# Down projection of a conv-gated FFN: fourteen of twenty-two tiles as seven block products

## The chip, the cores and the metric

The kernel runs on one core of a Trainium2 chip. The metric is device time in microseconds from launch to end, lower is better; it is given as the median of three runs. One further execution was taken with the hardware profiler, and every duration below that is not such a median is from it.

## The reference, cut to what matters

A two-layer encoder trunk over 1040 frames (16 learned ones ahead of 1024) of width 1024, all in float32. Each layer is an attention part (gated linear attention and softmax attention) and a gated FFN with a causal convolution of width 3. The change is in the FFN's last product:

```python
def conv_ffn(x, w_up, conv_w, conv_b, w_down):
    h = x @ w_up
    L = h.shape[1]
    hp = jnp.pad(h, ((0, 0), (CONV_W - 1, 0), (0, 0)))
    hc = conv_b
    for j in range(CONV_W):
        hc = hc + hp[:, j:j + L] * conv_w[j]
    u, g = jnp.split(hc, 2, axis=-1)
    return (jax.nn.silu(g) * u) @ w_down
...
        h = h + conv_ffn(rms_norm(h, ffn_norm[i]), w_up[i], conv_w[i], conv_b[i], w_down[i])
    return rms_norm(h, final_norm)[:, N_META:]
```

The FFN's inner width is 22 x 128 = 2816. The last layer needs only the last 1024 frames of the down projection.

## The kernel before, in words

Everything is held transposed: 128 channels on the partitions, frames along the row. A float32 product is three matmuls (`mm3`, L212): every operand is split into a rounded part `hi` and a remainder `lo`, and the passes are hi x hi (L216), lo x hi (L217) and hi x lo (L218). The rounded part is a copy on ScalarE (ACT), the remainder a subtraction on VectorE (DVE): for plain weights in `weights` (L183, L185), for activations in `split` (L330, L331). The first pass of a weight needs its `hi` alone, the second needs its `lo`.

The up projection (`ffn_up`, L1017) already is made of block products. Frames are cut in two halves, channels in two halves, and a pair of output tiles (an `u` and a `g` tile) with the two halves of the frames is a two by two block product, done by Winograd's form with seven products in place of eight. Each product has a weight factor (A11, A12, A21, A22 or a sum of them: S1, S2 and the changed A21, A12), made in `up_operand` and split in `up_split` (L1013, L1014), and an activation factor made once per layer. A product is 4 k tiles x 3 passes x 2 column blocks = 24 matmuls of 260 columns (258 in layer 1), into a PSUM tile of two banks. `evacuate` (L1180, L1181) copies or adds products into `u` and `g`; after the seventh, `conv` (L1169, L1173) and the gate (L1198, L1202) make the tile's activation, which POOL's queue stores to DRAM as `actd[j]` (L1203).

The down projection before is plain. `FGROUPS` cuts the 22 k tiles in groups of 5, 5, 5, 4 and 3. For each group but the last, `stream` goes over the eight output tiles m, loading and splitting the weights one tile ahead, and `dense3` makes the product into PSUM tiles of one bank, in chunks of 400, 384 and 256 frames (two of 512 in layer 1). DVE adds each chunk to the residual tile `hT[m]` (L1249), which was loaded from DRAM (`hm`) at the start of the stage (L1363) and stays on chip. `load_act` (L1231) loads an activation from `actd` and splits it. Ten are loaded while the last up tile's products run, by `during_last`, the others two groups ahead. The last group of three (`down_last`, L1261) goes chunk by chunk and feeds the next layer's norm, or the output.

Tiles as wide as a row come from a pool of 33 slots (`Slots`, L54), with six more in the FFN and some of the down stage. A slot is handed out again in the order in which slots were given back; whoever writes a slot next waits until its last user, a transfer included, is done.

PE's order is the order in which the program is written (`manual_schedule`, for PE alone). For the other engines and the queues a scheduler sets the order when the program is built. Each engine and each queue then works strictly in its order: an instruction that waits holds back those behind it.

Of the kernel before, what the change touches and what calls it, by code (L numbers as in the profile page):

```python
# [23 lines left out]
T = META + SEQ  # L24
# [8 lines left out]
CH_DOWN = [(16, 512), (528, 512)]  # L33
CTILES = [(0, 4), (4, 7), (7, 9)]
FT, NT, FIRST = 116, 9, 112
CH_FOX = [(0, 344), (344, 348), (692, 348)]
# [17 lines left out]
class Slots:  # L54
# [22 lines left out]
    def put(self, *slots):  # L77
        for s in slots:
            self.free.append(s.id)
# [53 lines left out]
class Kern:  # L133
# [843 lines left out]


    def up_operand(self, lyr, j, p, fw, raws, odd):
        nc = self.nc  # L980
        if j == 2 and p in (1, 2):
            src = fw.tile([128, 4, 128], F32, tag="raw2", name="raw2")
            nc.sync.dma_start(src[:], self.wm[lyr, M_UP + 4][:, 4 * p - 4:4 * p, :])
            return self.up_split(src, fw, odd)
        if j not in raws:
            u, g = self.wm[lyr, M_UP + 2 * j], self.wm[lyr, M_UP + 2 * j + 1]
            q = raws[j] = {}
            for name, src, k0, own in (("A11", u, 0, True), ("A21", g, 0, False), ("A22", g, 4, False), ("A12", u, 4, True)):
                q[name] = self.wp.tile([128, 4, 128], F32, tag="raw", name="raw", bufs=4) if own else \
                    fw.tile([128, 4, 128], F32, tag="raw2", name="raw2")  # L990
                nc.sync.dma_start(q[name][:], src[:, k0:k0 + 4, :])
        q = raws[j]

        def combine(out, a, b, op):
            if out not in q:
                q[out] = fw.tile([128, 4, 128], F32, tag="raw2", name="raw2")
            nc.vector.tensor_tensor(out=q[out][:], in0=q[a][:], in1=q[b][:], op=op)
# [8 lines left out]
        return self.up_split(src, fw, odd)  # L1006

    def up_split(self, src, fw, odd):
# [4 lines left out]
        nc.scalar.copy(hi[:], src[:])  # L1013
        nc.vector.tensor_tensor(out=lo[:], in0=src[:], in1=hi[:].bitcast(F32), op=ALU.subtract)  # L1014
        return [(hi[:, k, :], lo[:, k, :]) for k in range(4)]

    def ffn_up(self, lyr, mix, hT, pp, fw, halves, o0, during_last):  # L1017
        nc, s = self.nc, self.slots
# [218 lines left out]
        s.put(t)  # L1237
        acts[j] = (ah, al)

    def down_tiles(self, lyr, hT, pp, o0, dchunks, acts):  # L1240
        nc, s = self.nc, self.slots

        def down(i, m):
            g0, ng = FGROUPS[i]

            def f(w):
                def ev(ps, c0, n):
                    h = hT[m][:, c0:c0 + n]
                    nc.vector.tensor_tensor(out=h, in0=ps, in1=h, op=ALU.add)  # L1249
                self.dense3(pp, w, [acts[j] for j in range(g0, g0 + ng)], dchunks, ev)  # L1250
                if m == KD - 1:
                    for j in range(g0, g0 + ng):
                        s.put(*acts.pop(j))
                    if i + 2 < len(FGROUPS):
                        a, b = FGROUPS[i + 2]
                        for j in range(a, a + b):
                            self.load_act(j, o0, acts)
            return (self.wd[lyr, m][:, g0:g0 + ng, :], f)
        return [down(i, m) for i in range(len(FGROUPS) - 1) for m in range(KD)]

    def down_last(self, lyr, hT, pp, dchunks, acts, at_end, es):  # L1261

        nc, s = self.nc, self.slots
        g0, ng = FGROUPS[-1]
        w, held = [], []
        for m in range(KD):
            if m % 2 == 0:
# [55 lines left out]
    def run(self):  # L1323
# [17 lines left out]
        for lyr in range(DEPTH):  # L1341
            last = lyr == DEPTH - 1
            chunks = CH_LAST if last else CH
            mix, hT = self.attention(lyr, nm, hsrc, chunks, feed)
            o0 = CH_OUT[0][0] if last else 0
            dch = CH_OUT if last else CH
            acts, early = {}, {1: 2, 6: 2, 2: 1, 7: 2, 5: 1, 4: 1, 3: 1}

            def during_last(p):
                for _ in range(early[p]):  # L1350
                    self.load_act(len(acts), o0, acts)
# [82 lines left out]
```

## Time and profile before

| | us |
|---|---|
| median of three runs | 2647.05 |
| lowest and highest | 2646.37, 2649.61 |
| the profiled execution | 2645.09 |
| its span, first to last instruction | 2643.3 |
| mean granted TensorE clock | 0.987 |
| layer 0: first matmul of the down stage, first of its last group | 1071.76, 1288.92 |
| layer 1: the same | 2380.23, 2591.48 |

PE is TensorE's matmuls, PEld its weight loads, DVE VectorE, ACT ScalarE, POOL GpSimd, SP SyncE, whose queue issues most loads. In the busy times, a count follows each engine. In the groups of instructions a row is: line, engine, operation, output <- inputs, shapes, count | busy us, mean ns of one | idle time of the engine before them and what ended it. In the timeline a row is: start, duration in us, engine, line, operation, tiles, count, and in brackets the idle time before with what ended it. Matmuls overlap, so a matmul's own duration says less than the distance between the starts of two.

### The profile page before, as it was taken

Reading aid. Unit: us, or ns where it says so; the run is one execution under the profiler, and the core shown is the slowest. Engines: PE = TensorE matmul, PEld = TensorE weight load, DVE = VectorE, ACT = ScalarE, POOL = GpSimd, SP = SyncE. Lnnn points to the kernel's source line nnn. Section 1 sums busy time; section 2 is a strip of 40 time slices with the busy share of each in tenths; the row PEclk is TensorE's granted clock in tenths of the full one; section 3 lists DMA queues with packets and bytes.
Section 4 is the critical chain, followed back from the end, with each engine's and each line's share of the span. In section 5 each row is a group of like instructions: output and inputs, shape, how many; then the busy total and the mean of one; then the engine's idle time right before and its main releaser. Section 6 shows DMA issues by size and latency. Waiting matters only on the chain.

```text
span 2643.3 us, 46336 instructions
## 1 busy us (share of the span) xinstructions
PE 2523.9 (95%) x18102; PEld 2407.2 (91%) x18102; DVE 1759.9 (67%) x3484; ACT 1240.1 (47%) x2677; POOL 457.9 (17%) x596
## 2 busy tenths in 40 slices
PE   8999999897999999999999999998989999999997
PEld 7988898897999999999999888887889999998886
DVE  7655676759877777643665666666698767776335
ACT  6345665645544445421343565665455444453112
POOL 4033333333000000000201333332320000000002
PEclk9999999998999999999999999999999999999999
DMA  3222124341222222632312222142512222245222
GB/s 125 65 83 70 47 83 124 106 131 58 97 81 76 85 77 92 217 94 58 103 56 65 75 72 74 56 138 91 158 51 85 83 81 77 83 139 189 65 55 77
DMA packets 114476, 240.72 MB, mean 91 GB/s; under 512 B 14432, under 2 KB 36192, under 8 KB 114256
## 3 DMA queue, kind: packets, MB, share of 16 engines
q1 hardware_dynamic: 96000, 182.27, 22.7%
q0 software_dynamic: 16384, 53.18, 5.5%
q8 instruction: 142, 2.33, 0.4%
q10 hardware_dynamic: 1872, 2.31, 0.2%
q14 instruction: 78, 0.64, 0.1%
HBM read 174.01 MB, written 50.91 MB: 85 GB/s over the span
## 4 chain that ended last, share of the span: by engine, by line
PE 77%; DVE 13%; ACT 4%; issue 3%; DMA 2%; POOL 2%; DVEq 0%; SPq 0%; POOLq 0%; ACTq 0%
PE mm L216 12%; PE mm L217 12%; PE mm L218 12%; PE up L216 10%; PE up L217 10%; PE up L218 10%; PE av L706 2%; PE tr L688 2%; DVE S L655 1%; DVE x L1038 1%; PE wo L217 1%; PE wo L216 1%; PE wo L218 1%; DVE PT L331 1%; ACT P L667 1%
## 5 line engine op out<-in xcount | busy, mean ns | idle before, releaser
L216 PE MATMUL up<-x,hi 128*128 128x260 f32 (+1 forms) x2464 | 701.3, 285 | 22.7 <-DVE hu L1180 20.3
L217 PE MATMUL up<-x,lo 128*128 128x260 f32 (+1 forms) x2464 | 699.2, 284 | 0.0
L218 PE MATMUL up<-x,hi 128*128 128x260 f32 (+1 forms) x2464 | 698.5, 283 | 0.0
L216 PEld LDWEIGHTS up<-x,hi 128*128 128x128 f32 x2464 | 467.5, 190 | 24.4 <-DVE hu L1180 20.7
L217 PEld LDWEIGHTS up<-x,lo 128*128 128x128 f32 x2464 | 467.9, 190 | 0.1
L218 PEld LDWEIGHTS up<-x,hi 128*128 128x128 f32 x2464 | 467.8, 190 | 0.0
L216 PE MATMUL mm<-xh,hi 128*128 128x348 f32 (+4 forms) x1056 | 365.1, 346 | 0.0
L218 PE MATMUL mm<-xl,hi 128*128 128x348 f32 (+4 forms) x1056 | 340.9, 323 | 0.0
L217 PE MATMUL mm<-xh,lo 128*128 128x348 f32 (+4 forms) x1056 | 340.8, 323 | 0.0
L1014 DVE TENSOR_TENSOR lo<-raw,hi 128x512 fp32r<-128x512 f32 x308 | 212.9, 694 | 146.2 <-ACT hi L1013 146.2
L183 ACT CAST hi<-raw 128x512 fp32r<-128x512 f32 (+1 forms) x264 | 142.3, 543 | 329.8 <-PE mm L218 240.0
L217 PE MATMUL mm<-ah,lo 128*128 128x400 f32 (+1 forms) x760 | 266.4, 351 | 0.2 <-DVE lo L185 0.2
L218 PE MATMUL mm<-al,hi 128*128 128x400 f32 (+1 forms) x760 | 265.9, 350 | 0.0
L216 PE MATMUL mm<-ah,hi 128*128 128x400 f32 (+1 forms) x760 | 265.8, 350 | 0.0
L185 DVE TENSOR_TENSOR lo<-raw,hi 128x512 fp32r<-128x512 f32 (+1 forms) x196 | 120.7, 620 | 181.1 <-ACT hi L183 177.5
L1013 ACT CAST hi<-raw 128x512 fp32r<-128x512 f32 x308 | 190.3, 620 | 107.6 <-PE up L218 92.7
L216 PEld LDWEIGHTS mm<-xh,hi 128*128 128x128 f32 x1056 | 201.0, 190 | 6.0 <-issue 5.3
L217 PEld LDWEIGHTS mm<-xh,lo 128*128 128x128 f32 x1056 | 200.9, 190 | 0.4 <-issue 0.3
L218 PEld LDWEIGHTS mm<-xl,hi 128*128 128x128 f32 x1056 | 199.9, 189 | 0.4 <-issue 0.3
L1203 POOL DMA_DIRECT2D actd<-cv x44 | 23.4, 533 | 830.0 <-DVE cv L1202 830.0
L667 ACT ACTIVATE P<-S,m 116x460 f32<-116x460 f32 (+2 forms) x224 | 124.8, 561 | 76.9 <-DVE m L655 72.6
L331 DVE TENSOR_TENSOR PT<-tr,PT 116x464 fp32r<-116x464 f32 (+3 forms) x240 | 122.1, 516 | 55.8 <-ACT PT L330 54.1
(248 smaller groups left out, 5269.0 us busy)
## 6 DMA issues: line engine op xcount, KB each, us to landing
raw<-in_wm_dram SPq DMA_DIRECT2D x328, 256.0 KB, 2.6
raw<-in_wd_dram SPq DMA_DIRECT2D x64, 256.0 KB, 2.6
actd<-cv POOLq DMA_DIRECT2D x22, 520.0 KB, 2.9
st<-actd SPq DMA_DIRECT2D x22, 520.0 KB, 4.9
actd<-cv POOLq DMA_DIRECT2D x22, 512.0 KB, 3.0
st<-actd SPq DMA_DIRECT2D x22, 512.0 KB, 4.8
cb<-cd SPq DMA_DIRECT2D x16, 520.0 KB, 4.2
kA<-kA SPq DMA_DIRECT2D x24, 260.0 KB, 3.8
```

Of the source, the lines that this page charges most:

```text
L183: nc.scalar.copy(hi[:, :n, :], raw[:, :n, :])
L185: eng.tensor_tensor(out=lo[:, :n, :], in0=raw[:, :n, :], in1=hi[:, :n, :].bitcast(F32), op=ALU.subtract)
L216: nc.tensor.matmul(ps, wh, xh[:, c0:c0 + n], start=first, stop=False, skip_group_check=more)
L217: nc.tensor.matmul(ps, wl, xh[:, c0:c0 + n], start=False, stop=False, skip_group_check=more)
L218: nc.tensor.matmul(ps, wh, xl[:, c0:c0 + n], start=False, stop=last, skip_group_check=more)
L331: nc.vector.tensor_tensor(out=lo, in0=src, in1=hi.bitcast(F32), op=ALU.subtract)
L655: nc.vector.tensor_tensor_reduce(out=S[:rows, :n], in0=S[:rows, :n], in1=cb[:rows, c0:k1], scale=1.0, scalar=(BIG if ci == 0 else m[:rows, ...
L667: nc.scalar.activation(P[:rows, :n], S[:rows, :n], AF.Exp, scale=-1.0, bias=m[:rows, nch - 1:nch], accum_out=(den if nch == 1 else d3[:row ...
L688: nc.tensor.transpose(tr[:w, j, :rows], P[:rows, o:o + w], id_)
L706: nc.tensor.matmul(av[:, a:width], w.rearrange("p a b -> p (a b)"), x, start=(t == 0 and i == 0), stop=(t == last and i == 1))
L1013: nc.scalar.copy(hi[:], src[:])
L1014: nc.vector.tensor_tensor(out=lo[:], in0=src[:], in1=hi[:].bitcast(F32), op=ALU.subtract)
```

## The change

The fourteen k tiles 3 to 10 and 13 to 18 of the down projection are computed as block products, in two groups of eight and six tiles (`"s"`). Between them two groups of plain tiles remain (`"n"`: 0 to 2 and 11, 12), and the last group, 19 to 21.

- A block group takes pairs of output tiles, the group's first and second half of k tiles, and the two halves of the frames. `block_operand` is `up_operand` made general: four loads of weights, four sums, seven splits a pair. `down_blocks` issues the products in a written order, with the weight factors made four products ahead. A product has 4 (or 3) k tiles x 3 passes x 2 column blocks.
- The seven activation factors of a group are made by `prepare`, a generator that goes on whenever enough slots are free (`pump`, called after each product and each plain tile, and in the last up tile). For each two k tiles of a half it loads four slots, makes four sums and seven splits. The activations of the plain groups are loaded by the same generator.
- All this runs inside the pools of the up stage, with its four PSUM tiles of two banks. A plain tile is now two halves of the frames, each two column blocks of 260 (256 in layer 1), copied from PSUM by ACT into a slot.
- The residual stays in DRAM. Each plain output tile and each finished block tile is added to `hm` by a DMA that accumulates, issued on POOL's queue; `hT` is loaded after the last of them, for the last group.

```diff
-FGROUPS = [(0, 5), (5, 5), (10, 5), (15, 4), (19, 3)]
-HALVES, HALVES_LAST = (0, 520, 520), (8, 524, 516)
+GROUPS, LAST = (("n", 0, 3), ("s", 3, 8), ("n", 11, 2), ("s", 13, 6)), (19, 3)
+HALVES, HALVES_LAST, HALVES_OUT = (0, 520, 520), (8, 524, 516), (16, 528, 512)
...
+    def prepare(self, halves, acts, X):
...
+            nk = ng // 2
+            X[g0] = {p: [] for p in range(1, 8)}
+            for k0 in range(0, nk, 2):
+                m = min(2, nk - k0)
...
+                yield 2 + m
+                a0, a1 = load(g0, 0), load(g0, 1)
+                put(1, a0)
+                yield 2 + m
+                b0, b1 = load(g0 + nk, 0), load(g0 + nk, 1)
+                put(2, b0)
+                yield 1 + m
+                tt(a1, b1, a1, ALU.subtract)
+                t2 = get("t2")
+                tt(t2, a1, a0, ALU.add)
+                put(6, t2)
+                yield m
+                tt(a0, b1, t2, ALU.subtract)
+                put(5, a0)
...
+                put(7, a1)
...
+                tt(b0, b0, t2, ALU.subtract)
...
+                put(4, b0)
...
+                put(3, b1)
+    def pump(self, keep):
+        s = self.slots
+        while self.need + keep <= len([i for i in s.free if i not in s.lent]):
+            self.need = next(self.prep)
...
+    def down_blocks(self, lyr, g0, ng, X, pp, fw, halves, first):
+        seq = [(0, 1)]
+        for j in range(NP):
+            seq += [(j, 2), (j, 6), (j, 5), (j, 7)] + ([(j + 1, 1)] if j + 1 < NP else []) + [(j, 4), (j, 3)]
...
+            elif p == 4:
+                copy(q["g"][:, t0])
+                nc.gpsimd.dma_start(self.hm[2 * j + 1][:, o0:T], q["g"][:, o0:T], accum_op=ALU.add)
+                s.put(q["g"])
+            elif p == 3:
+                add(q["u"][:, t1], q["x"])
+                nc.gpsimd.dma_start(self.hm[2 * j][:, o0:T], q["u"][:, o0:T], accum_op=ALU.add)
+                s.put(q["u"])
...
+    def ffn_down(self, lyr, pp, fw, halves, acts, X, ids):
...
+                for h in range(2):
+                    ps = pp.tile([128, 2, 512], F32, tag=f"p{(2 * m + h) % 4}", name="down", bufs=1)
+                    for k in range(ng):
+                        for c in range(2):
+                            self.mm3(ps[:, c, :n], w[k], acts[g0 + k], halves[h] + c * n, n, k == 0, k == ng - 1)
...
+                        nc.scalar.copy(x, ps[:, :, :n])
+                if kind == "n":
+                    nc.gpsimd.dma_start(self.hm[m][:, o0:T], out[:, o0:T], accum_op=ALU.add)
+                    s.put(out)
...
+                self.pump(3)
...
-                    self.ffn_up(lyr, mix, hT, pp, fw, HALVES_LAST if last else HALVES, o0, during_last)
+                    self.ffn_up(lyr, mix, hT, pp, fw, HALVES_LAST if last else HALVES, o0, lambda p: self.pump(3))
+                    hT = self.ffn_down(lyr, pp, fw, halves, acts, X, ids)
...
-                    hT = [s.get(F32, f"h{k}", first=ids) for k in range(KD)]
-                    for k in range(KD):
-                        nc.sync.dma_start(hT[k][:, o0:T], self.hm[k][:, o0:T])
-                    self.stream(self.down_tiles(lyr, hT, pp, o0, CH_DOWN if last else CH, acts))
```

More of the change, by code (lines that the diff above doesn't have):

```diff
@@ L996, in combine @@
                 q[out] = fw.tile([128, 4, 128], F32, tag="raw2", name="raw2")
-            nc.vector.tensor_tensor(out=q[out][:], in0=q[a][:], in1=q[b][:], op=op)
+            nc.vector.tensor_tensor(out=q[out][:, :nk, :], in0=q[a][:, :nk, :], in1=q[b][:, :nk, :], op=op)
         if p == 6:
@@ new lines, in ffn_down, with load_residual, plain @@
+    def ffn_down(self, lyr, pp, fw, halves, acts, X, ids):
+        nc, s = self.nc, self.slots
+        o0, W = halves[0], halves[2]
+        n = W // 2
+        two = lambda ap: ap.rearrange("p (a b) -> p a b", b=n)
+        hT = []
+        def load_residual():
+            for k in range(KD):
+                hT.append(s.get(F32, f"h{k}", first=ids))
+                nc.sync.dma_start(hT[k][:, o0:T], self.hm[k][:, o0:T])
+        def plain(kind, g0, ng, m):
+            def f(w):
+                out = hT[m] if kind == "r" else s.get(F32, "do")
+                for h in range(2):
+                    ps = pp.tile([128, 2, 512], F32, tag=f"p{(2 * m + h) % 4}", name="down", bufs=1)
+                    for k in range(ng):
+                        for c in range(2):
+                            self.mm3(ps[:, c, :n], w[k], acts[g0 + k], halves[h] + c * n, n, k == 0, k == ng - 1)
+                    x = two(out[:, halves[h]:halves[h] + W])
+                    if kind == "r":
+                        nc.vector.tensor_tensor(out=x, in0=ps[:, :, :n], in1=x, op=ALU.add)
+                    else:
+                        nc.scalar.copy(x, ps[:, :, :n])
+                if kind == "n":
+                    nc.gpsimd.dma_start(self.hm[m][:, o0:T], out[:, o0:T], accum_op=ALU.add)
+                    s.put(out)
@@ L1253, in f @@
                         s.put(*acts.pop(j))
[L1254 to L1257, printed above, removed]
+                self.pump(3)
             return (self.wd[lyr, m][:, g0:g0 + ng, :], f)
-        return [down(i, m) for i in range(len(FGROUPS) - 1) for m in range(KD)]
+        i = 0
+        while i < len(GROUPS):
+            kind, g0, ng = GROUPS[i]
+            i += 1
+            if kind == "r":
+                if not hT:
+                    load_residual()
+                tiles = [plain(kind, g0, ng, m) for m in range(KD)]
+                while i < len(GROUPS) and GROUPS[i][0] == "r":
+                    tiles += [plain(*GROUPS[i], m) for m in range(KD)]
+                    i += 1
+                self.stream(tiles)
+            elif kind == "n":
+                tiles = [plain(kind, g0, ng, m) for m in range(KD)]
+                if i < len(GROUPS) and GROUPS[i][0] == "s":
+                    self.stream(tiles[:-1])
+                    w = self.weights(tiles[-1][0])
+                    _, a, b = GROUPS[i]
+                    i += 1
+                    self.down_blocks(lyr, a, b, X[a], pp, fw, halves, lambda: tiles[-1][1](w))
+                else:
+                    self.stream(tiles)
+        if not hT:
+            load_residual()
+        while any(j not in acts for j in range(LAST[0], sum(LAST))):
+            self.need = next(self.prep)
+        return hT
     def down_last(self, lyr, hT, pp, dchunks, acts, at_end, es):
         nc, s = self.nc, self.slots
-        g0, ng = FGROUPS[-1]
+        g0, ng = LAST
         w, held = [], []
@@ L1346, in run @@
             dch = CH_OUT if last else CH
[L1347 to L1351, printed above, removed]
+            acts, X = {}, {}
+            halves = HALVES_OUT if last else HALVES
+            self.prep = self.prepare(halves, acts, X)
+            self.need = next(self.prep)
             with tc.tile_pool(name=f"ffn{lyr}", bufs=1, reuse_waits="tile") as fp, \
```

108 lines of the change are left out of this document (90 added, 18 removed).

## The prediction

> **What bounds the kernel now.** I read the busy times first, then the granted clock and the busy time of three stretches, then the hand-over from the up stage to the down stage in order of time.
>
> ```profile
> PE 2523.9 (95%) x18102; PEld 2407.2 (91%) x18102; DVE 1759.9 (67%) x3484; ACT 1240.1 (47%) x2677; POOL 457.9 (17%) x596
> PE 77%; DVE 13%; ACT 4%; issue 3%; DMA 2%; POOL 2%; DVEq 0%; SPq 0%; POOLq 0%; ACTq 0%
> ```
>
> ```profile
> core 0: us, PE busy (x) PEld busy (x) DVE busy (x) ACT busy (x) POOL busy (x), PEclk, DMA share, GB/s
> 700.00:1000.00 300.00, 300.00 (x2507) 300.00 (x2506) 220.09 (x284) 144.51 (x209) 7.97 (x15) 1.00 0.24 80
> 1071.76:1288.92 217.16, 216.93 (x1370) 216.62 (x1369) 98.65 (x181) 49.19 (x82) 0.53 (x1) 1.00 0.33 102
> 2380.23:2591.48 211.25, 211.25 (x915) 171.55 (x913) 96.24 (x147) 47.95 (x80) 0.53 (x1) 1.00 0.32 98
> ```
>
> The first stretch is block products of the up stage in layer 0; the next two are the nineteen tiles of the down projection that the change rewrites, from their first matmul to the last group's first. PE is idle 0.23 us in them and has the full clock, while DVE is busy 98.65 of 217.16 us. So the down stage costs what its matmuls cost, and fewer matmul columns are worth their time, as long as PE stays fed.
>
> ```profile
> 1071.64 0.28 PE L218 MATMUL up<-x,hi 128*128 128x260 f32 x1
> 1071.76 0.34 PE L216 MATMUL mm<-ah,hi 128*128 128x400 f32 x1
> 1072.34 0.45 PE L217 MATMUL mm<-ah,lo 128*128 128x400 f32 x1 [0.23 <-DVE lo L185]
> ```
>
> At the hand-over PE waits 0.23 us, for the weight remainder (L185) of the first down tile. This is the wait to watch: the second matmul of each weight needs it.
>
> **The matmul stream.** A block product's matmul takes 300/2507 = 0.1197 us from start to start at 260 columns. For the 256 columns of layer 1:
>
> ```profile
> 1288.57 0.28 PE L216 MATMUL mm<-ah,hi 128*128 128x256 f32 x1
> ...
> 1288.92 0.35 PE L216 MATMUL mm<-ah,wl 128*128 128x400 f32 x1
> ```
>
> Three matmuls in 0.35 us, so 0.118 or a little less. After the change the five plain tiles of the middle groups issue 5 x 8 x 3 x 4 = 480 matmuls a layer, and the two block groups 28 products x (4+3) tiles x 3 passes x 2 column blocks = 1176; 1656 in all. Layer 0: 1656 x 0.1197 = 198.2 against 217.16, so -19.0. Layer 1: 1656 x 0.118 = 195.4 against 211.25, so -15.8. Together -34.8 us. That is all the change can gain: an eighth of fourteen tiles' columns, less what is lost by four narrow matmuls in place of two wide ones in layer 1. The last group of three tiles is the same.
>
> **The hand-over from up to down.** The seven factors of the first block group (fourteen splits and eight sums of activations) are made on DVE and ACT as slots come free. The built program shows where: in each layer DVE's order puts sixteen long operations between its last add of the up stage and the weight remainder of the first plain tile: eleven splits and sums of the preparation, the four convolution steps of the last feed-forward tile, and its gate product. The second matmul of the down stage needs that remainder, and PE's order is fixed, so PE stands until DVE has passed them all. Prices:
>
> ```profile
> L1180 DVE TENSOR_TENSOR hu<-up,hu 128x520 f32<-128x520 f32 x44 | 30.5, 692 | 0.8 <-PE up L218 0.8
> L185 DVE TENSOR_TENSOR wl<-raw,wl 128x384 fp32r<-128x384 f32 x16 | 8.7, 557 | 18.0 <-ACT wl L183 17.8 <-PE mm L218 0.3
> L1202 DVE TENSOR_TENSOR cv<-cv 128x1040 f32<-128x1040 f32 x22 | 27.2, 1235 | 0.1
> ```
>
> ```profile
> 1056.94 1.24 DVE L331 TENSOR_TENSOR al<-st,ah 128x1040 fp32r<-128x1040 f32 x1
> 1058.09 1.30 DVE L1173 SCALAR_TENSOR_TENSOR cv<-hu,vec,cv 128x1039 f32<-128x1039 f32 x1
> 1059.31 0.68 DVE L1014 TENSOR_TENSOR lo<-raw,hi 128x512 fp32r<-128x512 f32 x1
> ```
>
> Back to back, a 1040-wide split takes 1.15 us from start to start and a convolution step 1.22; the gate product I take as a split (1235 ns against 1.24). From the last up matmul's end DVE needs 0.69 for the last add, 12 x 1.15 + 4 x 1.22 and 0.56: 19.9 us. It is also late. In the last three products (3 x 24 x 0.1197 = 8.6 us of PE) its order holds an ACT copy to wait for (0.59, below), two adds of 0.69 and eight preparation steps of 1.15: 11.2 us. So 2.6 late, 22.5 in all; PE has one matmul to do meanwhile: 22.4 us of waiting, in each layer, +44.8. The low bound is 19.9 a layer (DVE not late). The high bound is 27.3: one activation load that DVE's order needs comes late by its whole landing, 4.9 (below). In the kernel before, DVE made this remainder ahead of the convolution steps:
>
> ```profile
> 1071.60 0.69 DVE L185 TENSOR_TENSOR lo<-raw,hi 128x512 fp32r<-128x512 f32 x1
> ...
> 1075.91 2.63 DVE L1173 SCALAR_TENSOR_TENSOR cv<-hg,vec,cv 128x1039 f32<-128x1039 f32 x2
> ```
>
>
> The kernel before has a wait of this kind at the start of layer 0's up stage:
>
> ```profile
> 636.49 0.69 DVE L1038 TENSOR_TENSOR x<-h,x 128x520 fp32r<-128x520 f32 x1
> 637.10 0.69 DVE L1038 TENSOR_TENSOR x<-dd,x 128x520 fp32r<-128x520 f32 x1
> 637.71 0.69 DVE L1180 TENSOR_TENSOR hu<-up,hu 128x520 f32<-128x520 f32 x1
> ```
>
> ```profile
> 638.46 0.59 PE L216 MATMUL up<-x,hi 128*128 128x260 f32 x1 [10.25 <-DVE hu L1180]
> ...
> 643.82 0.42 PE L216 MATMUL up<-x,hi 128*128 128x260 f32 x1
> 644.04 0.33 PE L217 MATMUL up<-x,lo 128*128 128x260 f32 x1
> 644.21 0.28 PE L218 MATMUL up<-x,hi 128*128 128x260 f32 x1
> ```
>
> An evacuation stood behind splits of operands and PE waited 10.25 us for it. It shows the second price too: after the wait the matmuls come 0.22 us apart until 644.04, at half clock, and 5.6 us at half speed lose 2.8. Two waits: +5.6 us. The Trainium skill (TensorE: Matmul & The Clock Gate, Part 1) gives an idle window of about 3.4 us for the drop to half; by it the shorter waits below would drop the clock as well, an estimated 1.7 us each. No run here shows that, and my sum leaves it out.
>
> **Accumulating transfers.** The residual stays in DRAM: every plain and block output is added to it by a transfer from POOL's queue, 32 a layer of 520 KB, and the slot that holds the output is free only when it has landed. The trace before has no such transfer. Nearest rows:
>
> ```profile
> actd<-cv POOLq DMA_DIRECT2D x22, 520.0 KB, 2.9
> st<-actd SPq DMA_DIRECT2D x22, 520.0 KB, 4.9
> h<-hm SPq DMA_DIRECT2D x8, 520.0 KB, 8.5
> ```
>
> A plain store of this size lands in 2.9 us, a load in 4.9, the slowest class in 8.5. An accumulate has the old bytes to read and the new to write: 2.9 if both overlap, 7.8 if one follows the other. I take L = 6 and keep 2.9 and 8.5 as ends. The Trainium skill (DMA: Bandwidth & Descriptors, Anatomy of one DMA) fits POOL's transfers as 2.0 us plus bytes over 436 GB/s, 3.2 us here against the 2.9 measured; with the bytes counted twice it gives an estimate of 4.4, and the sum below would be 16 us less.
>
> What waits for them stands in order behind other work on ACT, DVE and SP:
>
> ```profile
> L330 ACT CAST ah<-st 128x1040 fp32r<-128x1040 f32 x22 | 23.4, 1063 | 27.8 <-DMA st<-actd 25.8 <-DVE al L331 1.8
> L1181 ACT COPY hg<-up 128x520 f32<-128x520 f32 x44 | 26.1, 592 | 75.4 <-PE up L218 75.4
> L1013 ACT CAST hi<-raw 128x512 fp32r<-128x512 f32 x308 | 190.3, 620 | 107.6 <-PE up L218 92.7 <-DVE raw L997 7.7 <-PE wo L218 7.2
> ```
>
> In the first plain group: the output of m=3 is copied (0.59) and accumulated (L); into its slot SP loads an activation (4.9), ACT casts it (1.06), and behind that cast stands the copy of m=5 (0.59). Then m=5 is accumulated (L); into its slot DVE writes a split (1.24), behind which stand a weight remainder (0.69), SP's next activation loads (4.9), ACT's cast (1.06) and the copy of the first block product (0.59), whose PSUM bank the third product needs. That is 15.6 + 2L. PE covers eight half tiles of 18 matmuls and two products of 24: 17.2 + 5.7 = 22.9. Wait: 2L - 7.3, 4.7 us at L = 6, none at 2.9, 9.7 at 8.5. The second plain group repeats the pattern with its loads already made but only 12 matmuls a half tile; I give it the same price. Where the first block group ends, the last pair's copy (0.59), its accumulate (L), a cast into its slot (0.62), a split (0.69) and the add behind it (0.69) must pass while PE has one product and two half tiles, 5.7 us: L - 3.1, 2.9 at L = 6, none at 2.9, 5.4 at 8.5. Per layer 12.3 (0 to 24.8), both +24.6 us.
>
> **The rest.** SP loads the same bytes in halves. PSUM is four tiles of two banks; a plain half tile is copied by ACT in 0.59 while PE needs 2.15 for the next, so those copies hide unless ACT stands as above (each would then cost its 0.59). Added splits and sums away from the hand-over lie beside PE: a block pair has 14 DVE operations of 0.69 or less, 9.7 us, under 7 x 2.87 = 20.1 of PE. The residual is loaded after the last accumulates, L + 4.9, against eight PSUM tiles of cover; I take 1 us a layer, +2 (0 to 4).
>
> **Sum**, against the profiled execution's 2645.09 us (span 2643.3): -34.8 + 44.8 + 5.6 + 24.6 + 2 = +42.2, 2687.3. The median shown, 2647.05, lies 2.0 above that execution: 2689 us.
>
> **Rivals.** *The hand-over wait does not happen (faster).* If the remainder of the first plain tile were ready when PE comes, as the 0.23 us shows it before, the sum is -34.8 + 2 and 0 to 24.6: 2614 to 2639. It decides at 17.4 us of waiting a layer, half of the 34.8. Against it: the DVE order, which the 10.25 us wait shows to be kept, and sixteen operations that cannot take less than 19.9 us.
> *Accumulates are quick.* At L of 3.5 or less the queue waits are at most 0.4 a layer: 2647 - 34.8 + 50.4 + 2, about 2665 us. For it: DMA engines are a third busy (0.33).
> *Accumulates are slow.* At 8.5 the waits are 49.6: 2714; with DVE 4.9 us later in each layer and 4 for the tail 2726, and 2743 if each of the six shorter waits takes the clock down as the 10.25 us one did (2.8 each). Then the queue waits, and not the hand-over, are the main cost.
>
> **How the numbers follow.** About 0.2%, 5.3 us, is what a measurement of this kernel tells from no change. Forecast (L from 4 to 7) 0.44, slow accumulates 0.27, quick ones 0.22, no hand-over wait 0.05, the middle between (a wait of some 17 us) 0.02. Range: the low end takes 19.9 us twice, half the clock loss and no other wait, 2647 - 34.8 + 39.8 + 2.8 = 2655; the high end is the slow case with the clock, 2743, rounded to 2745. Faster 0.05, same 0.02, slower 0.93.
>
> **What would show it.** In the changed profile: two PE waits of 20 to 27 us for the weight remainder at the start of each down stage, with DVE busy through them and the clock at half behind them; matmuls of the block groups at 0.12 us; the accumulates' landing time in the DMA issues, near 6; waits of PE for ACT copies and DVE adds of 2 to 5 us around the plain groups. I am wrong if PE is not idle at the hand-over, or if its waits in the block groups exceed those two.

## The result, and the profile after

The changed kernel takes 2735.79 us (median of 4 runs, 2733.41 to 2744.22) against 2646.71 us beside it: 1.0342 times as long, 95% interval 1.0316 to 1.0367. It is slower, as forecast, and by 89 us where 42 were forecast. The time lies inside the range that was given, 2655 to 2745, near its upper end.

The busy times and the shares of the chain of waits, changed kernel:

```profile
span 2732.0 us, 48868 instructions
PE 2511.8 (92%) x19134; PEld 2427.7 (89%) x19134; DVE 1826.5 (67%) x3528; ACT 1345.7 (49%) x2865; POOL 513.2 (19%) x660
...
PE 40%; issue 33%; DVE 14%; DMA 5%; ACT 5%; POOL 2%; SPq 0%; DVEq 0%; POOLq 0%; ACTq 0%
```

PE was 95% busy and is 92%: 120 us without work became 220. The windows view puts this into the two down stages (from the last matmul of the up stage to the first of the last group):

```profile
core 0: us, PE busy (x) PEld busy (x) DVE busy (x) ACT busy (x) POOL busy (x), PEclk, DMA share, GB/s
700.00:1000.00 300.00, 300.00 (x2507) 300.00 (x2506) 220.06 (x284) 144.57 (x209) 7.97 (x15) 1.00 0.25 80
1072.63:1333.11 260.48, 208.55 (x1659) 206.68 (x1658) 125.06 (x176) 101.06 (x171) 27.36 (x32) 0.90 0.59 139
2428.39:2679.17 250.78, 205.38 (x1659) 203.42 (x1658) 124.32 (x176) 99.23 (x170) 27.32 (x32) 0.92 0.61 141
```

In the stretch of the up stage nothing changed: PE is busy for all of the 300 us, with the same 2507 matmuls. The down stages grew from 217.16 and 211.25 us to 260.48 and 250.78; PE idles 52 and 45 us in them, the granted clock is 0.90 and 0.92 where it was 1.00, and the DMA engines are busy 0.6 of the time where it was a third. The waits of PE, sorted by what ended them (us in total, times, longest), with those of the down stages:

```profile
PE down L218 <- DVE lo L186: 52.5, 2, 27.0
PE down L217 <- ACT du L1333: 18.5, 4, 8.2
PE down L217 <- DVE du L1332: 11.3, 2, 5.8
PE down L217 <- ACT do L1401: 10.9, 4, 5.2
...
PE down L217 <- ACT dg L1333: 2.9, 4, 0.9
PE down L217 <- DVE dg L1332: 1.1, 2, 0.9
```

The first row is the hand-over, once a layer; the others are waits for the copies and adds of outputs, 44.7 us. The hand-over of layer 0, in order of time, PE and then DVE (start, duration):

```profile
1072.76 0.28 PE L217 MATMUL down<-ah,hi 128*128 128x260 f32 x1
1100.05 0.58 PE L218 MATMUL down<-ah,lo 128*128 128x260 f32 x1 [27.02 <-DVE lo L186]
```

```profile
1073.79 2.39 DVE L332 TENSOR_TENSOR x<-st,x 128x1040 fp32r<-128x1040 f32 x2 [2.65 <-ACT x L331]
...
1080.16 0.69 DVE L1184 TENSOR_TENSOR hu<-up,hu 128x520 f32<-128x520 f32 x1
1080.77 1.23 DVE L332 TENSOR_TENSOR x<-st,x 128x1040 fp32r<-128x1040 f32 x1
1081.92 1.29 DVE L1177 SCALAR_TENSOR_TENSOR cv<-hg,vec,cv 128x1039 f32<-128x1039 f32 x1
...
1095.98 3.54 DVE L332 TENSOR_TENSOR x<-st,x 128x1040 fp32r<-128x1040 f32 x3
1099.44 1.49 DVE L186 TENSOR_TENSOR lo<-raw,hi 128x384 fp32r<-128x384 f32 x3
```

From 1080.77 to 1099.44 stand the sixteen operations; they took 18.7 us, as summed. But DVE's last add of the up stage came only at 1080.16.

The accumulating transfers and the weight loads of the down stage (KB each, median us from issue to landing):

```profile
raw<-in_wd_dram SPq DMA_DIRECT2D x64, 192.0 KB, 4.4
hm<-do POOLq DMA_DIRECT2D x16, 520.0 KB, 8.1
raw<-in_wd_dram SPq DMA_DIRECT2D x32, 256.0 KB, 4.3
hm<-do POOLq DMA_DIRECT2D x16, 512.0 KB, 7.0
...
hm<-dg POOLq DMA_DIRECT2D x8, 520.0 KB, 6.0
hm<-du POOLq DMA_DIRECT2D x8, 520.0 KB, 7.1
```

By these medians an accumulate lands in 5.4 to 8.1 us, and weight loads that took 2.6 us take 4.3. What hangs on a landing is seen on ACT and then DVE, where the first block group begins:

```profile
1139.60 0.59 ACT L1401 COPY do<-down 128x520 f32<-128x520 f32 x1
1151.37 1.06 ACT L331 CAST x<-st 128x1040 fp32r<-128x1040 f32 x1 [11.18 <-DMA st<-actd]
1152.33 0.58 ACT L1333 COPY du<-down 128x520 f32<-128x520 f32 x1
```

```profile
1142.31 1.24 DVE L332 TENSOR_TENSOR al<-st,ah 128x1040 fp32r<-128x1040 f32 x1 [4.50 <-DMA hm<-do]
```

ACT does nothing for 11.18 us. DVE stands 4.50 us until an accumulate has landed, because a split goes into its slot; behind that split stand weight remainders, behind those in SP's order a weight load, and behind that the load (issued at 1144.61) of the activation that ACT is to cast next. The copy of the first block product stands behind that cast. Its bank is what PE needs; PE resumes at 1152.97, 8.5 us after its last matmul began. This is the chain that the prediction wrote down for the first plain group.

### The profile page after: what moved, and what is told of

Same layout as the page of the kernel before. It is cut to its first block, busy times and chain, and to the rows that moved or that the text cites. A ratio compares the mean times of both kernels' runs of the same rounds, so it can differ in the third digit from the quotient of the medians.

```text
span 2732.0 us, 48868 instructions
## 1 busy us (share of the span) xinstructions
PE 2511.8 (92%) x19134; PEld 2427.7 (89%) x19134; DVE 1826.5 (67%) x3528; ACT 1345.7 (49%) x2865; POOL 513.2 (19%) x660
## 4 chain that ended last, share of the span: by engine, by line
PE 40%; issue 33%; DVE 14%; DMA 5%; ACT 5%; POOL 2%; SPq 0%; DVEq 0%; POOLq 0%; ACTq 0%
PE mm L217 6%; PE mm L219 6%; PE mm L218 6%; PE down L217 3%; PE down L219 3%; PE down L218 3%; PE av L707 2%; PE tr L689 2%; DVE S L656 1%; DMA raw<-in_wd_dram 1%; PE up L217 1%; PE up L218 1%; PE up L219 1%; DVE x L1042 1%; PE wo L218 1%
## 5 line engine op out<-in xcount | busy, mean ns | idle before, releaser
L217 PE MATMUL up<-x,hi 128*128 128x260 f32 (+1 forms) x2464 | 700.4, 284 | 22.8 <-DVE hu L1184 20.4
L1018 DVE TENSOR_TENSOR lo<-raw,hi 128x512 fp32r<-128x512 f32 (+1 forms) x420 | 281.9, 674 | 231.5 <-ACT hi L1017 231.3
L1017 ACT CAST hi<-raw 128x512 fp32r<-128x512 f32 (+1 forms) x420 | 254.1, 606 | 198.6 <-PE up L219 93.1
L217 PE MATMUL down<-x,hi 128*128 128x260 f32 (+1 forms) x784 | 223.2, 285 | 22.6 <-ACT du L1333 18.5
L219 PE MATMUL down<-x,hi 128*128 128x260 f32 (+1 forms) x784 | 222.2, 283 | 0.0
L218 PE MATMUL down<-x,lo 128*128 128x260 f32 (+1 forms) x784 | 222.0, 283 | 0.0
L1001 DVE TENSOR_TENSOR raw<-raw,raw 128x512 f32<-128x512 f32 (+1 forms) x240 | 155.7, 679 | 53.2 <-DMA raw<-in_wd_dram 51.7
L217 PEld LDWEIGHTS down<-x,hi 128*128 128x128 f32 x784 | 149.2, 190 | 24.7 <-ACT du L1333 19.3
```

Of the source, the lines that this page charges most:

```text
L217: nc.tensor.matmul(ps, wh, xh[:, c0:c0 + n], start=first, stop=False, skip_group_check=more)
L218: nc.tensor.matmul(ps, wl, xh[:, c0:c0 + n], start=False, stop=False, skip_group_check=more)
L219: nc.tensor.matmul(ps, wh, xl[:, c0:c0 + n], start=False, stop=last, skip_group_check=more)
L1001: nc.vector.tensor_tensor(out=q[out][:, :nk, :], in0=q[a][:, :nk, :], in1=q[b][:, :nk, :], op=op)
L1017: nc.scalar.copy(hi[:, :nk, :], src[:, :nk, :])
L1018: nc.vector.tensor_tensor(out=lo[:, :nk, :], in0=src[:, :nk, :], in1=hi[:, :nk, :].bitcast(F32), op=ALU.subtract)
```

## The experiments

Each kernel's ratio is to runs of the kernel before that were taken beside it (medians 2646.7 to 2649.2 us). Stops are PE's time from one matmul's start to the next less 0.12, where it is over 0.5 us, in both down stages together; "half clock" is the time that PE works at a granted clock of 0.5 there, halved, so what it costs.

| kernel | median us | ratio to before (95%) | hand-over | other stops | half clock |
|---|---|---|---|---|---|
| changed | 2735.8 | 1.0342 (1.0316 to 1.0367) | 52.9 | 47.3 | 16.5 |
| e1 paced | 2687.1 | 1.0153 (1.0138 to 1.0168) | 0 | 51.8 | 15.2 |
| e2 stores | 2699.9 | 1.0200 (1.0185 to 1.0215) | 50.7 | 19.7 | 14.4 |
| e3 no transfers | 2682.6 | 1.0142 (1.0121 to 1.0163) | 51.4 | 10.9 | 8.6 |
| e4 paced, no transfers | 2637.6 | 0.9963 (0.9953 to 0.9973) | 0 | 18.6 | 6.7 |
| e5 residual on chip | 2639.7 | 0.9963 (0.9949 to 0.9977) | 0 | 14.6 | 5.1 |
| e6 on chip, six first | 2640.1 | 0.9976 (0.9961 to 0.9990) | 0 | 13.8 | 4.5 |
| e8 remainder on POOL | 2722.8 | 1.0277 (1.0262 to 1.0292) | 0 | 79.3 | 21.1 |
| e9 borders | 2631.2 | 0.9938 (0.9922 to 0.9954) | 0 | 6.1 | 0 |
| e9 borders, six first | 2631.7 | 0.9938 (0.9922 to 0.9954) | 0 | 7.8 | 2.9 |
| e10 warm | 2742.9 | 1.0360 (1.0338 to 1.0381) | (46.1 filled) | 52.2 | 20.4 |

The theory at the start: DVE's order at the hand-over and the landing of the accumulates are two separate causes, and the half clock follows both. The rivals: the work of the preparation itself is too much; traffic, not landing, is what costs.

**e1: the preparation is held back and paced.**

```diff
-        while self.need + keep <= len([i for i in s.free if i not in s.lent]):
+        while most and self.need + keep <= len([i for i in s.free if i not in s.lent]):
+            if acts is not None and len(acts) == GROUPS[0][2]:
+                return
...
-lambda p: self.pump(3)
+lambda p: self.pump(3, acts=acts)
...
-                self.pump(3)
+                self.pump(3, 2)
```

(the last pair of lines is the call behind a plain tile; each step that is made takes one from `most`)

> Changed kernel, but in the up stage only the three activations of the first plain group are loaded, and the factors of the first block group are made in the first plain group, at most two steps of the preparation behind each plain tile. The computation is the same. My theory: the two hand-over waits (27.0 us and 25.5 us) are DVE's order and nothing else, so they go with their half clock (about 5 us together), and the plain tiles cover the preparation: 2735.8 - 52.5 - 5 = 2678 us, 2668 to 2692. Rival A, the wait only moves: DVE has the same 25 us of splits and sums to do, and PE meets them at the first block products (waits for x factors of 15 us or more a layer): 2710 to 2736. Rival B: the waits behind accumulating transfers grow, because slots are now asked for later: 2690 to 2715, with more than 50 us of PE waits for ACT copies and DVE adds of the down stage.

PE's waits in the down stages of e1:

```profile
PE down L217 <- ACT do L1404: 21.4, 5, 7.2
...
PE down L217 <- DVE du L1335: 12.4, 2, 7.1
PE down L217 <- ACT du L1336: 10.8, 4, 5.0
```

2687.1 us, 48.7 less than the changed kernel. The row of the hand-over is gone, and PE waits 1.5 us in all for factors: rival A falls. The other waits are 47.5 us in these rows and dg's, for 44.7, more of them now behind the copies of do; rival B asked for more than 50. The same sums and splits are done, only later; so the hand-over was the place of that work in DVE's order.

**e2: plain stores in place of accumulates.**

```diff
-nc.gpsimd.dma_start(self.hm[m][:, o0:T], out[:, o0:T], accum_op=ALU.add)
+nc.gpsimd.dma_start(self.hm[m][:, o0:T], out[:, o0:T])
```

(and the same for dg and du)

> Changed kernel, but the 64 accumulating transfers are plain stores of the same bytes to the same place; the residual's sum is left out, so this is for its time only. My theory: a store lands in about 3 us in place of 6 to 8, the waits behind the landing (PE for do, dg and du copies and adds, 43.6 us in the changed kernel) fall under 12 us, and with their half clock and some 5 us of the weight waits the time is about 2690 us, 2678 to 2702; the two hand-over waits stay at 25 to 28. Rival A, traffic and not landing: the stores load the DMA engines about half as much as the accumulates, so about half of it stays: 2705 to 2718. Rival B, the waits are of the preparation on DVE and ACT and of the slots, whatever the output does: 2728 to 2740.

PE's waits in e2, and below them its DMA issues:

```profile
PE down L218 <- DVE lo L186: 50.4, 2, 26.1
...
PE down L217 <- DVE du L1332: 8.2, 2, 4.4
PE down L217 <- ACT du L1333: 7.5, 2, 3.9
...
PE down L217 <- ACT dg L1333: 2.7, 4, 0.7
```

```profile
raw<-in_wd_dram SPq DMA_DIRECT2D x64, 192.0 KB, 3.0
hm<-do POOLq DMA_DIRECT2D x16, 520.0 KB, 3.8
```

2699.9 us, 35.9 less. The queue and the slots are those of the changed kernel, and DVE, ACT, POOL and SP issue the same operations in the same order; the landing of a do falls from 8.1 to 3.8 us, and 44.7 us of waits to 18.4. That is more than the 12 expected. The time lies inside the range given and below the 2705 to 2718 of the rival by traffic.

**e3: no output transfers**, their three lines left out; the slots are put back as before.

> Changed kernel, but the 64 output transfers of the block and plain groups are left out and their slots are free at once; this is for its time only. My theory: as with plain stores, the waits behind landings go, and the weight loads come back from 4.4 to about 2.6 us: 2735.8 - 60 = 2676 us, 2664 to 2690, within 12 us of the plain stores. If traffic is what costs, it is 15 us or more below the plain stores. If the waits are of the preparation, it is 2725 to 2740 like the changed kernel. The two hand-over waits of 25 to 28 us stay under every theory.

The waits other than the hand-over's, and the weight loads:

```profile
PE down L217 <- ACT dg L1333: 5.3, 4, 2.1
PE down L217 <- DVE du L1332: 4.7, 2, 2.5
```

```profile
raw<-in_wd_dram SPq DMA_DIRECT2D x64, 192.0 KB, 2.4
```

2682.6 us, 53.2 less than the changed kernel and 17.3 less than with stores: by the bound set beforehand (15 us or more) a plain store costs as well. The bound is met narrowly: the four runs of e2 lie between 2693.7 and 2701.8 us, those of e3 between 2677.3 and 2691.5, and in e3 parts of the orders of DVE, ACT and SP differ too (105 of 3528 places on DVE). Whether a store costs by its landing or its traffic the two runs don't part; the weight loads fall from 3.0 to 2.4 us with it. The 10.0 us of waits that are left have nothing to do with these transfers. They lie where a block group ends. Half of them (5.3) are the last pair's: product 4 accumulates onto the bank from which the copy of product 7, just ahead of it, has still to read. In the other pairs a product of the next pair stands between the two. The others (4.7) come just behind the first block group, where a plain tile takes the bank of product 3, from which DVE has still to add.

**e4: e1 and e3 together.**

> Both edits: preparation in the plain group, and no output transfers; for its time only. What is left is the matmul stream. My theory: the before kernel's 2646.7 - 34.8 (1656 matmuls of the two middle parts a layer in place of the plain tiles' columns) + 5 to 15 for the preparation that is now beside the plain tiles: about 2622 us, 2612 to 2634, so below the kernel before. Rival: the narrower products cost more than 0.12 us a matmul or the block operands' sums hold PE up; then the stream gains nothing and the time stays at 2640 or more.

2637.6 us, 98.2 less than the changed kernel where the two edits alone give 48.7 and 53.2: they are two causes, and their sum, 101.9, is nearly reached. It is 3.6 above the range I gave: the paced preparation leaves a copy of a plain output late once a layer (3.3 us), and the borders cost as in e3. The rival (narrow products cost more) falls: stops and half clock left out, the stages take 199.1 and 196.1 us for 198.2 and 195.4 computed.

**e7: du's accumulates alone**, 16 of 64; the lines of do and dg are left out.

> Changed kernel with the accumulating transfers of du alone (16), those of do and dg left out; for the landing time. If an accumulate takes its 6 to 8 us because others and the weight loads press on the same DMA engines, a lone one lands near 3 to 4 us, as a store did (3.0 to 3.8). If the reading back and adding itself takes long, it lands at 5.5 us or more, as in the changed kernel (7.1 and 6.7). I expect 5.5 to 6.5.

Its DMA issues:

```profile
hm<-du POOLq DMA_DIRECT2D x8, 520.0 KB, 5.6
hm<-du POOLq DMA_DIRECT2D x8, 512.0 KB, 5.5
```

(2690.9 us in a single run.) With no other accumulates about, these still take 5.6 and 5.5 us where e2's stores of du, among other stores, took 3.0 and 3.7. So accumulating by itself costs at least 1.8 to 2.6 us. Among the other accumulates those of du took 7.1 and 6.6. Those of do, one for every plain tile of 4.3 or 2.9 us, took 7.0 and 8.1; no run has them alone.

**e8: one remainder on another engine.**

```diff
-eng = nc.gpsimd if self.att else nc.vector
+eng = nc.gpsimd if self.att or self.low else nc.vector
```

(`low` is set during the down stage)

> Changed kernel with one edit: the weight remainders of the down stage's plain tiles are made on POOL, which is idle there, in place of DVE; the preparation is where it was. If the order of DVE ahead of that one remainder were all there is to the hand-over, both waits go with their half clock: about 2678 us, as with the paced preparation. My theory: the remainder is only the first that waits. The copies of the first plain outputs on ACT stand behind casts of the preparation that wait for DVE's sums, and PE meets that two or three tiles later: a wait of 10 to 15 us a layer for ACT copies takes the place of the 25: 2703 to 2718 us.

PE's waits in e8:

```profile
PE down L217 <- ACT do L1401: 30.6, 8, 12.5
...
PE down L217 <- DVE hu L1184: 8.7, 2, 4.5
```

2722.8 us, 13.0 less than the changed kernel, above my range by 5. The wait for the remainder is gone, but PE runs into the next two: first the last add of the up stage (hu), then a copy that stands on ACT behind casts of the preparation, 12.5 us. So the hand-over is not the place of one instruction: the preparation as a whole must not be issued there.

**e5 and e6: the residual on chip.** Every product's half is added into the loaded residual by DVE; the preparation is paced by one step, the plain remainders are made on POOL.

```diff
-            if p == 1:
-                q["u"] = s.get(F32, "du")
-                copy(q["u"][:, t0])
+            u, g = hT[2 * j], hT[2 * j + 1]
+            if p == 1:
+                add(u[:, t0], q["a"])
...
-                nc.gpsimd.dma_start(self.hm[2 * j][:, o0:T], q["u"][:, o0:T], accum_op=ALU.add)
-                s.put(q["u"])
+                add(u[:, t1], q["x"])
...
-GROUPS = (("n", 0, 3), ("s", 3, 8), ("n", 11, 2), ("s", 13, 6))
+GROUPS = (("n", 0, 3), ("s", 3, 6), ("n", 9, 2), ("s", 11, 8))
```

(the last pair of lines is e6's alone)

> Same groups as the changed kernel (3 plain, 8 in blocks, 2 plain, 6 in blocks, 3 last), but the residual is loaded at the start of the down stage and every half of a block product or plain tile is added to it on chip by DVE: no accumulating transfers, no output slots, no ACT copies of outputs. The preparation is paced (one step behind each plain tile and block product), and the weight remainders of plain tiles are made on POOL. Same computation. My theory: hand-over wait, landing waits and most of the half clock go, and the stream's 34 us stay gained, less some 7 us a layer at the borders of the groups: 2646.7 - 34 + 14 + 4 = 2631 us, 2622 to 2642, faster than the kernel before. Rival: DVE, with 120 more adds from PSUM in the down stages, becomes what PE waits for, and the gain is eaten: 2645 to 2670.

> As the kernel with the residual on chip, with the block group of six ahead of the block group of eight (3 plain, 6 in blocks, 2 plain, 8 in blocks, 3 last). Same matmuls; the first group's factors are 21 slots in place of 28 and their preparation is shorter, so it fits under the first plain tiles. My theory: 2 to 5 us less than its sister: about 2628 us, 2618 to 2640. Rival: the border between the groups sets the loss, not the preparation: the same time as its sister within 2 us.

2639.7 and 2640.1 us. DVE is busy 164.25 of 206.89 us in layer 0's stage and does not become the bound; both are a little faster than the kernel before, by 0.4 and 0.2%. Three edits were made at once here, so what each is worth is not shown by these two runs. The order of the groups makes no difference to the time, as e6's rival had it: the border and not the preparation was next.

**e9: the border.** For the last pair of a block group another order of products:

```diff
-seq += [(j, 2), (j, 6), (j, 5), (j, 7)] + ([(j + 1, 1)] if j + 1 < NP else []) + [(j, 4), (j, 3)]
+seq += [(j, 2), (j, 6), (j, 5), (j, 7), (j + 1, 1), (j, 4), (j, 3)] if j + 1 < NP else \
+    [(j, p) for p in (6, 5, 7, 2, 4, 3)]
```

> The kernel with the residual on chip (same groups as the changed kernel), with one more edit: for the last pair of output tiles of a block group the products run in the order 6, 5, 7, 2, 4, 3, so that no product accumulates onto a PSUM bank in the step behind the one whose sum DVE still has to read from it. My theory: the waits of 2.7 and 2.9 us at the end of the first block group and 1.2 and 1.2 at the end of the second (PE for h, from DVE) go, about 8 us, and 2 windows of half clock with them, 3 us: 2639.7 - 11 = 2629 us, 2622 to 2637. Rival: the wait only passes to the next reader of a bank, the first plain tiles: 2636 to 2642.

> The same edit in the kernel with the group of six ahead of the group of eight. My theory: its border waits of 2.5 us go too, the 3.7 us at the second product stay: 2640.1 - 11 = 2629 us, 2620 to 2637. Rival: as for its sister, 2636 to 2642.

The windows of the first of the two, its down stages:

```profile
1076.43:1279.35 202.92, 199.91 (x1659) 199.07 (x1658) 163.38 (x227) 70.12 (x107) 13.30 (x14) 1.00 0.32 101
2384.73:2584.44 199.71, 197.16 (x1660) 196.53 (x1658) 162.50 (x227) 69.32 (x107) 13.90 (x14) 1.00 0.31 99
```

2631.2 us, 0.9938 of the kernel before (0.9922 to 0.9954), both orders alike. Here the stops at the borders are gone and the clock is 1.00 throughout: 202.92 and 199.71 against 217.16 and 211.25, so 25.8 of the 34.8 us that the narrower stream offers. The profiled execution took 2639.0 us, the longest of the six; the last section shows where most of the difference lies. By the ratio this version is 0.6% faster than the kernel before.

**e10: PE kept busy in the hand-over.** The changed kernel with 195 useless matmuls a layer where it waited:

```diff
+WARM = 195
...
+if g0 == m == 0:
+    ps = pp.tile([128, 2, 512], F32, tag="p0", name="warm", bufs=1)
+    for c in range(WARM):
+        nc.tensor.matmul(ps[:, c % 2, :n], w[0][0], acts[0][0][:, halves[0]:halves[0] + n], start=True, stop=True)
```

> Changed kernel, with 195 further matmuls of 260 (256) columns into an unread PSUM bank ahead of the first plain tile of each layer's down stage, where PE stood for 27.2 and 25.7 us: work of no use, to keep PE busy in the wait; 195 x 0.12 = 23.4 us. My theory of the clock: it falls because PE is idle, and a window at half speed behind a wait costs half of what PE is busy in it. PE's wait there falls to 2 to 5 us, the half clock behind it (6.0 us in layer 0 and 3.4 in layer 1) goes, and the time is 2735.8 - 4.7 = 2731 us, 2726 to 2736. Rival: the clock is lowered for another cause (the load of the other engines, or the time of the run), then it falls there with PE busy, the extra matmuls take 0.22 us each, 43 us, and the time rises by 15 us or more a layer.

The windows of these matmuls (the granted clock follows POOL's count):

```profile
1076.52:1099.80 23.28, 23.28 (x197) 23.28 (x195) 21.62 (x20) 13.32 (x14) 0.53 (x1) 1.00 0.20 64
2438.96:2461.81 22.85, 22.85 (x197) 22.85 (x195) 22.85 (x22) 12.08 (x12) 0.53 (x1) 1.00 0.14 49
```

With PE busy the clock stays at 1.00 through the same stretch of DVE's work, and a matmul takes 0.12 us: the rival falls, idleness lowers it. But the time is 2742.9 us, not 2731. In layer 0 a wait of 4.0 us was left behind the useless matmuls and took the clock down all the same, and the half clock in the two stages came to 20.4 us in all, where it was 16.5. In the profiled executions the two stages took 2.5 us more than in the changed kernel, and the rest, which the edit doesn't touch, some 9 more. The saving of 4.7 us is thus not shown in the time.

## Why the prediction was right in sign and wrong in size

By the terms of its sum, with the profiled executions (spans 2643.3 and 2732.0, so +88.7):

| term | predicted | measured |
|---|---|---|
| matmul stream | -34.8 | -34 |
| hand-over | +44.8 | +52.9 |
| half clock | +5.6 | +16.5 |
| queue waits | +24.6 | +47.3 |
| residual, last groups | +2 | +5.7 |
| sum | +42.2 | +88.4 |

**The stream** held. Stops and half clock left out, the stages take 198.5 and 196.0 us for 198.2 and 195.4 computed; e9, with no half clock in them, has 199.8 and 196.8, so a gain of 32 to 34.

**The hand-over** held as a mechanism: two waits for the remainder, sixteen operations ahead of it in 18.7 us. The step that was short is DVE's lateness: 2.6 us were given, and the last add ended 7.2 us after it could have begun and run (1080.85 for 1072.91 + 0.69). In the rows above DVE stands 2.65 us for an ACT cast of the preparation, and ACT had stood 2.76 us for a transfer before that cast; the sum left a late transfer to the upper bound. DVE also had two operations of 1.15 us more to do there than the eight steps counted: a ninth step, and the gate product of the tile before. 27.0 lies just inside the bound of 27.3.

**The queue waits** are the largest miss, +22.7, and the step that failed is the choice L = 6, with terms that the formula lacks. The landing was 5.4 to 8.1, and 8.1 where it counted most, in the plain groups. With 8.1 the formula gives 2 x 8.9 + 5.0 = 22.8 a layer, 45.6 for the 47.3 measured. That agreement is in part luck. By place the stops were, in layer 0 and 1: up to the first block product 9.9 and 10.3 us (4.7 each in the sum), at the end of the first block group 3.1 and 1.7 (2.9), in the second plain group 11.4 and 8.0 (4.7), at the end of the second block group 1.9 and 0.8 (nothing). The formula also has no wait left at the landing of a store, and e2 and e3 show 19.7 and 10.9 us there. Its border term goes by the landing alone, and left out the waits for banks of PSUM that e3 shows with no transfer at all (10.0 us; with the residual on chip e9 removed the like). The slow rival, given 0.27, was nearer to what happened: its last figure, 2743, is built from 49.6 us of queue waits, a hand-over 9.8 longer and 16.8 of half clock behind short waits, beside 47.3, 8.1 and 11.8 measured. The Trainium skill (DMA: Bandwidth & Descriptors, Anatomy of one DMA) has 2.0 us plus bytes over 436 GB/s, 3.2 us for these 520 KB; the stores of e2 (3.0 to 3.8) lie around it. The estimate of 4.4 for an accumulate lies below all rows here, the lone 5.5 and 5.6 included.

**The half clock** is the other miss, +10.9. Behind the hand-over it cost 4.7 us, for 5.6. The failed step is that the sum put it at nothing behind the shorter waits, where it cost 11.8, with the reason that no run showed it. That reason doesn't hold: the trace of the kernel before has ten stretches at half clock, and eight of them follow waits of 1.6 to 3.3 us. One in the attention of layer 1, the matmul behind the wait and then the window (PEclk 0.50):

```profile
1682.09 0.45 PE L681 MATMUL tr<-ident,Ps 116*116 116x116 f32 x1 [3.32 <-DVE PT L331]
```

```profile
1681.77:1685.18 3.41, 3.09 (x11) 2.92 (x12) 2.37 (x7) 1.06 (x5) 0.56 (x1) 0.50 0.31 102
```

In the changed kernel, layer 0's second plain group:

```profile
1241.85 0.58 PE L217 MATMUL down<-ah,hi 128*128 128x260 f32 x1 [5.83 <-DVE du L1332]
1242.24 0.42 PE L218 MATMUL down<-ah,lo 128*128 128x260 f32 x1
...
1246.06 0.28 PE L218 MATMUL down<-ah,lo 128*128 128x260 f32 x1
1246.18 0.29 PE L219 MATMUL down<-al,hi 128*128 128x260 f32 x1
```

A wait of 5.8 us, then 4.2 us of matmuls 0.22 apart, then 0.12 again. The Trainium skill (TensorE: Matmul & The Clock Gate, Part 1) had the rule that I set aside: an idle window of about 3.4 us drops the clock. With half of such a window, an estimated 1.7 us, behind each of six shorter waits the term would have been 15.8, near the 16.5 measured. That too is partly luck, as the sum's waits of 2.9 us are shorter than a window and would not have dropped the clock by that rule.

**The residual and last groups** took 38.4 and 36.0 us for 34.0 and 34.7: PE waits there for remainders of the last weights, made on DVE. With no transfers (e4) the two take 35.4 and 35.9 us, so most of layer 0's excess comes with them, and layer 1's does not.

**The rivals.** Without the hand-over wait (e1) the kernel is still slower, by 40 us: the rival that gave 2614 to 2639 allowed at most 24.6 us of queue waits and no half clock, and e1 has 51.8 and 15.2. With quick landings (e2, 3.0 to 3.8) it takes 2700, not 2665: the stops left there (19.7), more half clock (14.4 for 5.6) and the longer hand-over (50.7 for 44.8) make up the difference.

## What to carry to other kernels

Before work is prepared "as slots come free", count what the in-order engine must pass at the stage's border: the stall is that queue, and moving a single instruction off it (e8) only moves the stall. A result that is accumulated in DRAM holds its buffer longer than one that is stored (5.6 us for 3.0 alone, up to 8.1 here). Where another in-order queue needs the buffer, adding on chip, with an engine that has room, takes that chain away (e5, which paces the preparation as well). Look through the trace before the change for half clock behind short waits, price each wait of PE above some 2 us with its share of it, and look for the border case in an order of products that is clean only inside its loop (e9).

## What the runs showed of the hardware that was not expected

The half clock comes in whole steps: every stretch inside the changed kernel is 3.41 us or a multiple (6.83, 10.24, up to 30.72), save the last at its end, and all changes of the clock from 54.68 us on lie on one grid of 3.413 us, within 0.005 us. Of PE's stops besides the hand-overs in the down stages of the changed kernel and of e1 to e4, all sixteen from 3.8 to 8.3 us were followed by a stretch, seven of ten between 2.2 and 3.5, none of 2.0 or less; in e5 one of 1.9 was. The Trainium skill (TensorE: Matmul & The Clock Gate, Part 1) calls the window free-running and 3413 ns long; the steps agree.

What decides is how much of one window PE stands idle. Cut into windows of 3.41 us from each change of the clock, the thirteen traces show it. PE was busy for less than 1.5 us in 162 windows at full clock, and half clock followed every one. Between 1.5 and 2 us it followed 26 of 110. With 2 us or more it followed 7 of 7625; these seven are all at the same work in the attention of layer 1, with PE busy throughout, and stay unexplained. So about half a window of idleness is enough in these runs: a wait of 3.8 us always fills half of some window, and a shorter one does or doesn't by where it falls. That is less than the whole idle window of the rule cited above.

That moves parts that no edit touches. The attention of layer 1, from the end of layer 0's last group to the first product of layer 1's up stage, in the kernel before and in e9:

```profile
1322.90:1920.58 597.68, 558.55 (x3993) 525.02 (x3992) 388.00 (x1059) 312.27 (x862) 173.96 (x239) 0.99 0.29 86
```

```profile
1314.64:1925.04 610.40, 568.67 (x3992) 534.75 (x3991) 390.77 (x1063) 314.18 (x867) 175.68 (x241) 0.97 0.28 85
```

The same matmuls take 12.7 us more at a mean clock of 0.97. The changed kernel had 597.68 there too, e5 606.52 in its profiled execution. Waits of about 2 us are frequent in that part, and how many windows they bring down differs: two stretches at half clock, 10.2 us in all, in the kernel before, and seven, 34.1 us, in e9. Whether an edit upstream settles it or chance does was not tried.
